# Row softmax on one core: two instruction-alignment directives moved behind the first pass, and the last two tiles divided and stored ahead of the next maximum

## The chip, the cores and the metric

One core of a Trainium2 chip runs the whole program. The metric is the device time of one execution in microseconds. The span of a profile (first to last event of the program) is about 1.8 us shorter than the time of the same execution: 315.6 against 317.42 us for the kernel before. A profile is of one execution, not of the median one.

## The reference

`x` is 32 x 512 x 1024 in float32, `temperature` is 0.5.

```python
scaled = x / temperature
shifted = scaled - np.max(scaled, axis=-1, keepdims=True)
exp_x = np.exp(shifted)
return (exp_x / np.sum(exp_x, axis=-1, keepdims=True)).astype(np.float32)
```

Each of the 16384 rows of 1024 numbers is read once and written once: 67.1 MB in, 67.1 MB out.

## The kernel before

The rows are cut into 16 tiles of 128 partitions x 8 rows (4.19 MB each), in six buffers. A tile is worked on in two groups of four rows. VectorE takes the maxima and later multiplies by the reciprocal of the sums; ScalarE takes the exponentials and sums them up as it goes; SyncE issues the loads, ScalarE's queue issues the stores. A buffer's next load is issued when its store has landed.

```python
def exponential(g): ...          # 4 activations on ScalarE, each with its row sums
def divide(g):
    nc.vector.reciprocal(recip, sums)
    for b in range(k):           # k = 4
        nc.vector.tensor_scalar_mul(
            tiles[i][:, a + b, :], in0=tiles[i][:, a + b, :], scalar1=recip[:, b : b + 1]
        )
def store(g):                    # only after a tile's second group
    ...
        nc.scalar.dma_start(out=dram(of, i)[:, a : a + k, :], in_=tiles[i][:, a : a + k, :])
        ... load()               # the tile six further on

with tc.manual_schedule():
    nc.vector.addr_align(128, offset=0, max_nops=0)
    nc.scalar.addr_align(128, offset=0, max_nops=0)
    for _ in range(BUFS):        # 6
        load()
    for g in range(len(groups) + 1):
        if g < len(groups):
            maximum(g)
            exponential(g)
        if g > 0:
            divide(g - 1)
            store(g - 1)
```

The division of a group stands behind the maximum of the next, so that ScalarE has its exponentials done by then. `addr_align` computes nothing: it asks that the next instruction of that engine lie at a multiple of 128 instruction slots. With `max_nops=0` the padding in front of it is jumped over.

Of the kernel before, what the change touches and what calls it, by code (L numbers as in the profile page):

```python
# [1 line left out]

# [4 lines left out]



TILES = [[8]] * 16  # L10
BUFS = 6

GROUP = 4


@with_exitstack
def kernel(
    ctx: ExitStack,
    tc: tile.TileContext,
    x: bass.AP,  # L20
    temperature: bass.AP,
    out: bass.AP,
):
    nc = tc.nc
    f32 = mybir.dt.float32
    scale = 1.0 / float(temperature)
    extreme = mybir.AluOpType.max if scale > 0 else mybir.AluOpType.min

    P = 128
    xf = x.flatten_outer_dims()  # L30
    of = out.flatten_outer_dims()
    n, d = xf.shape
    assert sum(sum(ks) for ks in TILES) * P == n

    data = ctx.enter_context(tc.tile_pool(name="data", bufs=BUFS))
    stats = ctx.enter_context(tc.tile_pool(name="stats", bufs=4))


    groups, first, r = [], [], 0
    for i, ks in enumerate(TILES):  # L40
        first.append(r)
        r += sum(ks)
        a = 0
        for k in ks:
            for b in range(0, k, GROUP):
                m = min(GROUP, k - b)
                groups.append((i, a + b, m, (a, k) if b + m == k else None))
            a += k

    def dram(t, i):  # L50
        k = sum(TILES[i])
        block = t[P * first[i] : P * (first[i] + k), :]
        return block.rearrange("(p k) d -> p k d", p=P, k=k)

    tiles, small = [], []

    def load():
        i = len(tiles)
        if i < len(TILES):
            xt = data.tile([P, sum(TILES[i]), d], f32, name="xt")  # L60
            nc.sync.dma_start(out=xt, in_=dram(xf, i))
            tiles.append(xt)

    def maximum(g):
        i, a, k, _ = groups[g]
        top, bias, sums, recip = (
            stats.tile([P, k], f32, name=name) for name in ("top", "bias", "sums", "recip")
        )
        small.append((bias, sums, recip))
        nc.vector.tensor_reduce(  # L70
            out=top, in_=tiles[i][:, a : a + k, :], axis=mybir.AxisListType.X, op=extreme
        )
        nc.vector.tensor_scalar_mul(bias, in0=top, scalar1=-scale)  # L73

    def exponential(g):
        i, a, k, _ = groups[g]
        bias, sums, _ = small[g]
        for b in range(k):
            nc.scalar.activation(  # L79
                tiles[i][:, a + b, :],  # L80
                tiles[i][:, a + b, :],
                mybir.ActivationFunctionType.Exp,
                bias=bias[:, b : b + 1],
                scale=scale,
                accum_out=sums[:, b : b + 1],
            )

    def divide(g):
        i, a, k, _ = groups[g]
        _, sums, recip = small[g]  # L90
        nc.vector.reciprocal(recip, sums)  # L91
        for b in range(k):
            nc.vector.tensor_scalar_mul(  # L93
                tiles[i][:, a + b, :], in0=tiles[i][:, a + b, :], scalar1=recip[:, b : b + 1]
            )

    def store(g):
        i, _, _, part = groups[g]
        if part:
            a, k = part  # L100
            nc.scalar.dma_start(out=dram(of, i)[:, a : a + k, :], in_=tiles[i][:, a : a + k, :])
            if a + k == sum(TILES[i]):
                load()



    with tc.manual_schedule():

        nc.vector.addr_align(128, offset=0, max_nops=0)
        nc.scalar.addr_align(128, offset=0, max_nops=0)  # L110
        for _ in range(BUFS):
            load()
        for g in range(len(groups) + 1):
            if g < len(groups):
                maximum(g)
                exponential(g)
            if g > 0:
                divide(g - 1)
                store(g - 1)


# [1 line left out]
_INS = ['x', 'temperature']  # L123
_OUTS = [((32, 512, 1024), 'float32')]

_NUMBERS = {'temperature': 0.5}


# [26 lines left out]
```

## Time and profile before

| | kernel before |
|---|---|
| median time | 317.71 us of 3 runs (317.61 to 318.15) |
| span of the profile | 315.6 us |
| VectorE busy | 235.5 us, 75% |
| ScalarE busy | 149.6 us, 47% |
| moved by DMA | 134.26 MB, 425 GB/s over the span |

How to read it: the two busiest engines leave a quarter and a half of the span idle, while the DMA row of the page stands at 90% or more in every slice but the first and the last. The queues tell what the bytes are:

```profile
DMA packets 4613, 134.26 MB, mean 425 GB/s; under 512 B 512, under 2 KB 512, under 8 KB 512
q1 hardware_dynamic: 2304, 67.11, 49.7%
q10 hardware_dynamic: 2304, 67.11, 49.2%
q14 instruction: 5, 0.04, 0.0%
```

The columns of a queue are packets, MB and the share of 16 DMA engines' time. q1 has the loads, q10 the stores. q14 is the fetch of the program's own instructions, five packets of 8 KB. They take 0.0% of the DMA engines' time.

### The profile page before, as it was taken

How to read it: one execution, taken by the hardware profiler on the slowest of the kernel's cores; microseconds unless marked ns; L12 is line 12 of the kernel's file. 1: busy time of each engine (PE TensorE's matmuls, PEld its weight loads, DVE VectorE, ACT ScalarE, POOL GpSimd, SP SyncE). 2: the span in 40 equal slices, each digit the busy share in tenths (PEclk: the TensorE clock that was granted, in tenths of full speed). 3: DMA queues.
4: the chain of work that ended last, by engine and by line, in shares of the span. 5: the costliest groups of instructions: out<-in, count | busy, mean ns of one | idle time of the engine just before them, and what ended most of it. 6: DMA issues, size and time to landing. Idle time of an engine off the chain costs nothing.

```text
span 315.6 us, 622 instructions
## 1 busy us (share of the span) xinstructions
DVE 235.5 (75%) x224; ACT 149.6 (47%) x257; POOL 0.2 (0%) x4
## 2 busy tenths in 40 slices
DVE  0299999999789494994939949498594976949720
ACT  0176666666626255361553615546065560645500
POOL 0000000000000000000000000000000000000000
DMA  8999999999999999999999999999999999999996
GB/s 330 415 448 415 386 457 407 461 411 453 424 440 432 432 432 429 444 424 453 415 454 407 457 407 457 403 461 403 461 403 461 403 462 403 461 419 444 428 436 278
DMA packets 4613, 134.26 MB, mean 425 GB/s; under 512 B 512, under 2 KB 512, under 8 KB 512
## 3 DMA queue, kind: packets, MB, share of 16 engines
q1 hardware_dynamic: 2304, 67.11, 49.7%
q10 hardware_dynamic: 2304, 67.11, 49.2%
q14 instruction: 5, 0.04, 0.0%
HBM read 67.11 MB, written 67.11 MB: 425 GB/s over the span
## 4 chain that ended last, share of the span: by engine, by line
DVE 72%; another core or an unknown queue 15%; DMA 4%; ACT 3%; issue 1%; DVEq 0%
DVE top L70 43%; DVE xt L93 27%; DMA xt<-in_x_dram 4%; ACT xt L79 3%; DVE recip L91 1%; DVE bias L73 1%; DVEq L150 0%
## 5 line engine op out<-in xcount | busy, mean ns | idle before, releaser
L79 ACT ACTIVATE xt<-xt,bias 128x1024 f32<-128x1024 f32 x128 | 145.4, 1137 | 136.0 <-DVE recip L91 118.6
L70 DVE TENSOR_REDUCE top<-xt 128x4 f32<-128x4096 f32 x32 | 141.3, 4416 | 62.2 <-DMA xt<-in_x_dram 62.2
L93 DVE TENSOR_SCALAR xt<-xt,recip 128x1024 f32<-128x1024 f32 x128 | 87.7, 749 | 1.1
L79 ACT ACTIVATION_READ_ACCUMULATOR xt<-xt,bias 128x1 f32 x128 | 23.8, 186 | 0.0
L79 ACT ACT_TABLE_LOAD x1 | 1.3, 1283 | 13.5 <-DMA xt<-in_x_dram 13.5
L91 DVE RECIPROCAL recip<-sums 128x4 f32<-128x4 f32 x32 | 5.5, 171 | 2.1 <-ACT xt L79 2.1
L73 DVE TENSOR_SCALAR bias<-top 128x4 f32<-128x4 f32 x32 | 5.5, 170 | 1.1
L136 POOL MEMSET const-bfloat16-1.0<- 128x1 bf16 x1 | 0.1, 102 | 0.0
L136 POOL MEMSET const-uint8-127<- 128x1 uint8 x1 | 0.1, 102 | 0.0
L136 POOL MEMSET const-float32-0.0<- 128x1 f32 x1 | 0.1, 99 | 0.2 <-issue 0.2
L136 POOL MEMSET const-float32-1.0<- 128x1 f32 x1 | 0.1, 99 | 0.0
## 6 DMA issues: line engine op xcount, KB each, us to landing
xt<-in_x_dram SPq DMA_DIRECT2D x16, 4096.0 KB, 50.2
out_dram<-xt ACTq DMA_DIRECT2D x16, 4096.0 KB, 38.4
```

Source lines behind the costliest of these rows:

```text
L70: nc.vector.tensor_reduce(out=top, in_=tiles[i][:, a : a + k, :], axis=mybir.AxisListType.X, op=extreme)
L73: nc.vector.tensor_scalar_mul(bias, in0=top, scalar1=-scale)
L79: nc.scalar.activation(tiles[i][:, a + b, :], tiles[i][:, a + b, :], mybir.ActivationFunctionType.Exp, bias=bias[:, b : b + 1], scale=scal ...
L91: nc.vector.reciprocal(recip, sums)
L93: nc.vector.tensor_scalar_mul(tiles[i][:, a + b, :], in0=tiles[i][:, a + b, :], scalar1=recip[:, b : b + 1])
L136: nc = _bacc.Bacc("TRN2", target_bir_lowering=False, num_devices=1)
```

## The change

The intent is twofold. The directives leave the head, where they stand ahead of all work, and come behind the first pass. And from tile 14 on, the second half of a tile is divided and stored before the next tile's maximum is taken: those stores go out earlier, and the last tile has no division between its two maxima.

```diff
+ALIGNED = 0
+ALONE = 14
...
     with tc.manual_schedule():
-        nc.vector.addr_align(128, offset=0, max_nops=0)
-        nc.scalar.addr_align(128, offset=0, max_nops=0)
         for _ in range(BUFS):
             load()
         for g in range(len(groups) + 1):
+            alone = g < len(groups) and groups[g][0] >= ALONE and groups[g][1] == 0
+            if g > 0 and alone:
+                divide(g - 1)
+                store(g - 1)
             if g < len(groups):
                 maximum(g)
                 exponential(g)
-            if g > 0:
+            if g > 0 and not alone:
                 divide(g - 1)
                 store(g - 1)
+            if g == ALIGNED:
+                nc.vector.addr_align(128, offset=0, max_nops=0)
+                nc.scalar.addr_align(128, offset=0, max_nops=0)
```

## The prediction

> **What bounds the kernel now.** I started with the page's time slices. The DMA row stands at 9 (90% or more) from the second slice to the next to last, while VectorE is 75% busy and ScalarE 47%. The DMA line under it gives 134.26 MB over the span, a mean of 425 GB/s, half read and half written. The first suspicion is therefore that transfers set the time and the engines only keep pace. Shares of busy time are averages, so I cut the trace into stretches at its two ends, each as long as one 4 MB tile takes (two calls; the columns are the stretch, its length, busy us of VectorE, ScalarE and GpSimd with counts, clock, DMA share, GB/s).
>
> ```profile
> DMA  8999999999999999999999999999999999999996
> ...
> 0.00:1.40 1.40, 0.00 (x0) 0.00 (x0) 0.20 (x4) 1.00 0.00 0
> 1.40:11.10 9.70, 0.00 (x0) 0.00 (x0) 0.00 (x0) 1.00 1.03 414
> 20.80:30.50 9.70, 9.38 (x11) 6.68 (x13) 0.00 (x0) 1.00 1.00 432
> 30.50:40.90 10.40, 10.33 (x12) 7.65 (x13) 0.00 (x0) 1.00 0.98 391
> 40.90:50.60 9.70, 9.63 (x8) 6.03 (x12) 0.00 (x0) 1.00 1.00 432
> ...
> 264.30:273.97 9.67, 9.60 (x8) 4.64 (x8) 0.00 (x0) 1.00 1.00 434
> 273.97:283.65 9.68, 5.12 (x8) 4.64 (x8) 0.00 (x0) 1.00 1.00 433
> 283.65:293.32 9.67, 9.60 (x8) 4.64 (x8) 0.00 (x0) 1.00 1.00 434
> 293.32:303.00 9.68, 6.64 (x12) 4.64 (x8) 0.00 (x0) 1.00 1.00 433
> 303.00:312.68 9.68, 0.00 (x0) 0.00 (x0) 0.00 (x0) 1.00 1.00 433
> 312.68:315.64 2.96, 0.00 (x0) 0.00 (x0) 0.00 (x0) 1.00 0.08 33
> ```
>
> What to see: the last column is 432 to 434 whether VectorE is busy 9.6 us of a stretch or not at all. A 4.19 MB tile, read or written, takes 9.67 us, and 32 such transfers in a row (16 loads, 16 stores) take 309.5 us. What the kernel spends above that is small: 1.4 us before the first byte, 0.7 us in the one slow stretch around the first store (10.4 instead of 9.7 us), some 0.5 us of slow start in the stretch before it at 414 GB/s, and some 3 us from the last byte to the span's end. The sum is 315 us, against a span of 315.6.
>
> Then the waits, to see whether the engines or the transfers are late:
>
> ```profile
> DVE top L70 <- DMA xt<-in_x_dram: 62.2, 12, 13.4
> ```
>
> VectorE stands idle for data 62.2 us in 12 waits; after the first (13.4 us) these are some 4.5 us, once per tile. The chain that ended last attributes 72% to VectorE, but it ends with the issue of the last store and follows VectorE back through its own instructions; it doesn't see that the transfers were full all the while. I trust the stretches over it.
>
> Last the tail, in order of time, because that is where the change acts:
>
> ```profile
> 262.90 4.42 DVE L70 TENSOR_REDUCE top<-xt 128x4 f32<-128x4096 f32 x1 [4.48 <-DMA xt<-in_x_dram]
> ...
> 270.41 0.34 ACTq L101 DMA_DIRECT2D out_dram<-xt  x1
> ...
> 282.25 4.42 DVE L70 TENSOR_REDUCE top<-xt 128x4 f32<-128x4096 f32 x1 [4.49 <-DMA xt<-in_x_dram]
> ...
> 289.76 0.34 ACTq L101 DMA_DIRECT2D out_dram<-xt  x1
> ...
> 302.01 0.34 ACTq L101 DMA_DIRECT2D out_dram<-xt  x1
> ```
>
> Tile 14 arrives at 262.9 and tile 15 at 282.25. The stores of tiles 13, 14 and 15 are issued at 270.41, 289.76 and 302.01. The completion records of the last four stores stand at 285.9, 295.5, 305.2 and 314.8: one every 9.6 to 9.7 us, the full rate. So when store 15 is issued at 302.01, store 14 still has 3.2 us to its completion. Store 15 completes 9.64 us after store 14: it followed without a gap. **This pair of numbers decides the prediction.**
>
> **The Trainium skill.** "DMA: Bandwidth & Descriptors", section Specifications, gives a fabric ceiling of 435 GB/s; the trace's 432 to 434 agrees, so no rearranged program moves these bytes faster. The same page, section "Queues, rings and completion order", says each DMA engine takes turns between the queues that have work, packet by packet. The trace agrees: the load and store queues have 49.7% and 49.2% of the engines' time, and with both filled a tile lands about every 19.4 us (262.9 to 282.25), twice 9.67. "Runtime: NRT & Kernel Launch", section "Instruction fetch mechanics", says instructions are refilled in 16 KiB blocks by DMA and that a taken branch out of the window stalls for a fetch. This trace shows 5 instruction packets with 0.04 MB in all, 8 KB each, so smaller pieces than the page's block; no view of the kernel before shows what such a branch costs.
>
> **The change, part by part.**
>
> *Alignment directives.* Two directives, one per engine, that compute nothing, move from ahead of all work to behind the first maximum and exponential. At the head their cost, if any, lies inside the 13.4 us wait for tile 0. In the new place VectorE meets its directive after the first bias (18.05 us) and ScalarE after its fourth exponential (22.6 us). What one costs there I can't read from this trace. From 13.4 to 84.8 us VectorE runs without a break and is behind the loads; a stall of d us moves the first store (33.1 us) by d. But six loads, 25.2 MB or 58 us of transfers, were queued at the start, so the transfers don't run dry; and VectorE catches up at its waits of 3.1 us (at 84.8) and then 4.5 us per tile. For d up to several us the cost is 0. Moving the directives may also move which engine fetches when, at about 0.3 us for one of 16 DMA engines: estimate 0 to 0.3 us either way.
>
> *Tiles 14 and 15: divide ahead of the maximum.* No instruction is added or removed; VectorE's order becomes max, divide, divide, max in place of max, divide, max, divide. Durations from the page's groups: maximum 4.42 (first after a wait) or 4.41, bias 0.17, reciprocal 0.17, four divisions 2.74 together; four exponentials 4.65 from the chain. Both reordered groups stand where VectorE idles 4.5 us for data.
> - Tile 13: its last exponentials run 255.66 to 260.3. Reciprocal and divisions follow at once, to 260.3 + 0.2 + 2.75 = 263.25; store 13 is issued about 263.3 and not at 270.41, 7.1 us earlier. The maximum of tile 14 starts at 263.3 instead of 262.9.
> - Tile 14: the two maxima end about 272.2, its exponentials at about 272.5 and 277.1, its second division at about 280.1. Store 14 is issued there, 9.6 us earlier than 289.76, and still before tile 15 lands, so the maximum of tile 15 starts at 282.25 as before.
> - Tile 15: between its two maxima there is no division now (0.17 + 2.74, minus small overlaps: 2.8 us). Second maximum 286.8 to 291.2, exponentials 287.0 to 291.5 and 291.5 to 296.1, last division to 299.2: store 15 issued about 299.2 and not 302.0, **2.8 us earlier**.
>
> On the path that sets the end: nothing. Store 13 joins a queue that still holds store 12 (until 285.9) and store 14 one that holds 12 and 13, so the DMA engines do the same work in the same order. Store 15 now waits about 6 us behind store 14 instead of 3.2, and completes at 314.8 again. Sum: 0 us from the reordering, -0.3 to +0.3 from the directives.
>
> **The rivals.**
> 1. *The tail is bound by compute.* Then the 2.8 us reach the end: 317.7 - 2.8 = 314.9, or 0.9% faster. For it: nothing but the long engine chain. Against it: the 433 GB/s stretch across 302 us and the 9.64 us between the last two completions.
> 2. *Earlier stores take bandwidth from the last loads.* Tile 15 would land later, at worst by part of the 7 us by which store 13 moves. Against it: the store queue wasn't empty at 263.3 in the kernel before, so it got its turn already; and even 3 us would be absorbed by the 2.8 us won.
> 3. *The directive stalls hard.* If an engine waits for a fetch through full DMA queues, each turn costs some 1.2 us (one 32 KB packet per engine at this rate, an estimate), so perhaps 2 to 6 us. VectorE has slack for this as shown; only over some 20 us would the transfers suffer. The end time would stay near 317.7.
> 4. *Fetch traffic shifts into or out of the tail.* A fetch of 0.3 us on the DMA engine that ends last moves the end by just that.
>
> **Range and chances.** The centre is the time before with a sliver off: 317.6. The three runs before spread over 0.54 us, and rivals 1 and 4 stretch the low side, a moderate stall and another chip the high side: 316.7 to 318.4. Faster by over 2% would need 6.4 us; above the 309.5 us of transfers there are only about 6 us in all, most of them start and completion. Slower by over 2% would need the transfers to stand idle 6.4 us, for which I see no mechanism but a very long stall. Chances 0.005, 0.985 and 0.01.
>
> **What would show it.** In the changed profile: stores issued near 263.3, 280.1 and 299.2 (reordering right); stretches to the end at 432 to 434 GB/s and the last two completions 9.6 to 9.7 us apart (bound right); tile 15 landing within 0.5 us of 282.25 (rival 2 wrong); an idle gap or none behind VectorE's 18 us and ScalarE's 22.6 us (cost of the directive), with the waits near 85 us shorter by that gap. I'd be wrong if the DMA share dropped in some slice after the first, or if the completion of the last store followed its issue by a constant 12.8 us, which would mean the tail had been the engines'.

## The result, and the profile after

The changed kernel takes 318.21 us (median of 6 runs, 317.52 to 318.31), the kernel before 317.60 us in the same rounds (6 runs, 317.43 to 318.15). The ratio is 1.0014 with a 95% interval of 1.0001 to 1.0027. Ratios here are the mean time of one kernel's runs over that of the other's of the same rounds, so they aren't quite the ratio of the medians quoted. Within 2% this is "the same"; the interval just leaves out 1, on the slow side.

Three views of the changed kernel answer those of the prediction. First the stretches (stretch, length, busy us of VectorE, ScalarE and GpSimd with counts, clock, DMA share, GB/s). A packet is counted whole in the stretch in which it starts, so a share of a short stretch can pass 1.00:

```profile
1.40:11.10 9.70, 0.00 (x0) 0.00 (x0) 0.00 (x0) 1.00 0.98 388
...
293.32:303.00 9.68, 5.05 (x9) 3.68 (x8) 0.00 (x0) 1.00 1.00 433
303.00:312.68 9.68, 0.00 (x0) 0.00 (x0) 0.00 (x0) 1.00 1.00 433
312.68:316.51 3.83, 0.00 (x0) 0.00 (x0) 0.00 (x0) 1.00 0.08 34
```

Up to 312.68 us the tail moves its bytes at 433 GB/s, as before. What has grown is the last row: 3.83 us in place of 2.96, at a share of 0.08. A share of 0.08 of 16 DMA engines says that on average little more than one of them was still at work. Then the tail in order of time:

```profile
263.92 4.41 DVE L74 TENSOR_REDUCE top<-xt 128x4 f32<-128x4096 f32 x1
264.04 0.34 ACTq L105 DMA_DIRECT2D out_dram<-xt  x1
...
280.81 0.34 ACTq L105 DMA_DIRECT2D out_dram<-xt  x1
283.12 4.42 DVE L74 TENSOR_REDUCE top<-xt 128x4 f32<-128x4096 f32 x1 [2.34 <-DMA xt<-in_x_dram]
287.65 4.41 DVE L74 TENSOR_REDUCE top<-xt 128x4 f32<-128x4096 f32 x1
300.02 0.34 ACTq L105 DMA_DIRECT2D out_dram<-xt  x1
```

The reordering works: the three stores go out at 264.0, 280.8 and 300.0, where they were at 270.4, 289.8 and 302.0. But tile 15 lands at 283.1, not 282.25. Third, a wait that the kernel before doesn't have (us in total, times, longest):

```profile
DVE top L74 <- issue: 0.4, 1, 0.4
```

That is VectorE at 17.75 us, where it meets its directive. ScalarE shows no such gap. The first store is still issued at 33.05 us (33.12 before), so the gap itself costs nothing. The views of `prof` leave branches out, but the packed traces have one branch record for each directive: at 0.72 and 0.76 us in the kernel before, at 17.59 us (VectorE) and 17.81 us (ScalarE) in the changed one, ten in the run `align_often` below, none in `no_align`, which has no directives.

**Following single DMA engines.** The last stretch asked which engine was late. The packet records give start, length and queue of each packet. In the steady part a DMA engine starts each 32 KB packet about 1.21 us after the one before, so I joined packets whose ends and starts meet into 16 chains, one per DMA engine. This is an inference, but a tight one: in all thirteen profiles the records can be joined so that each chain has 256 packets of 32 KB and, for each tile and queue, eight of them followed by one of 4 bytes. It shows:

- Before: 13 DMA engines end by 313.5 us, three at 314.3 to 314.5. Instruction packets after the start stand at 1.8, 3.6, 124.6, 162.3 and 253.3 us.
- After: 14 end by 313.7 us, two at 315.2 and 315.3. Instruction packets stand at 22.1, 22.1, 136.2, 163.1 and 260.2 us.
- An instruction packet of 8 KB holds its DMA engine for 0.31 us, and the data packet behind it is often slower, 1.33 to 1.82 us instead of 1.21. One fetch thus makes a DMA engine 0.4 to 0.9 us late. While the queues are full, that lag stays. Against the median of the 16, packet by packet, the latest DMA engine of the kernel before goes from 0.4 to 1.2 us at its fetch at 162.3 us and ends 1.2 us behind. In the changed kernel a DMA engine goes from 0.0 to 1.0 us at a fetch at 22.1 us, from 1.1 to 1.9 us at the one at 163.1 us, and ends 1.9 us behind.
- In every profile, whatever the kernel, the span ends 1.14 to 1.19 us after the last packet of a load or store on the latest DMA engine.

So the 0.87 us between the spans (316.51 and 315.64) are the lateness of one or two of 16 DMA engines. (The profile of the kernel before is of a run of 317.42 us, faster than each of the six timed ones, so the spans differ by more than the medians.) The experiments had to tell whether the moved fetches make it (theory A), or the early stores (theory B), or chance.

### The profile page after: what moved, and what is told of

It reads as the page before. It is cut to its first block, busy times and chain, and to the rows that moved or that the text cites. A ratio compares the mean times of both kernels' runs of the same rounds, so it can differ in the third digit from the quotient of the medians.

```text
span 316.5 us, 622 instructions
## 1 busy us (share of the span) xinstructions
DVE 235.8 (74%) x224; ACT 149.5 (47%) x257; POOL 0.2 (0%) x4
## 4 chain that ended last, share of the span: by engine, by line
DVE 69%; another core or an unknown queue 13%; ACT 7%; DMA 4%; issue 1%; DVEq 0%; ACTq 0%
DVE top L74 41%; DVE xt L97 25%; ACT xt L83 7%; DMA xt<-in_x_dram 4%; DVE bias L77 1%; DVE recip L95 1%; DVEq L160 0%; ACTq L83 0%
```

## The experiments

Eleven more runs were made, all of them correct and all within 2% of the kernel before. They came in three sets of rounds on three chips: the first four rows, the next four, the last three. Ratios are to be compared within a set first. The table has their times, each with the kernel before in the same rounds; the instruction packets of their profiles after 1 us; and the ends of the DMA engines.

| run | us (median, range) | before, us | ratio, 95% interval | instruction packets at us | most DMA engines end by; late ones |
|---|---|---|---|---|---|
| reorder_only | 317.78 (317.45 to 318.08) | 317.80 | 0.9998 (0.9986 to 1.0010) | 1.8, 3.9, 124.7, 162.7, 253.4 | 313.5; 314.5, 314.8 |
| align_only | 319.43 (318.21 to 321.14) | 317.80 | 1.0059 (1.0033 to 1.0085) | 22.1, 22.1, 136.9, 163.5, 260.9 | 314.3; 315.7, 316.0 |
| no_align | 317.90 (317.89 to 317.98) | 317.80 | 1.0003 (0.9991 to 1.0015) | 64.9, 65.0, 181.8, 240.1 | 313.8; 314.2, 314.8 |
| align_often | 321.08 (320.41 to 323.83) | 317.80 | 1.0124 (1.0093 to 1.0155) | ten: in pairs near 22, 66, 120, 180, 240 | 319.1; 320.9 |
| scalar_behind | 317.71 (317.65 to 318.06) | 317.65 | 1.0003 (0.9991 to 1.0015) | 4.1, 22.2, 135.7, 162.6, 259.7 | 313.5; 314.7, 314.8 |
| vector_behind | 318.54 (317.68 to 321.01) | 317.65 | 1.0042 (1.0015 to 1.0068) | 1.8, 22.2, 125.9, 165.5, 257.4 | 314.8; 318.1 |
| reorder_late | 317.96 (317.61 to 318.31) | 317.65 | 1.0008 (0.9996 to 1.0021) | as reorder_only | 313.7; 314.7, 315.0 |
| before_late | 317.96 (317.60 to 318.23) | 317.65 | 1.0007 (0.9995 to 1.0019) | as reorder_only | all 315.1 to 315.3 |
| before_later | 320.82 (320.70 to 321.26) | 317.82 | 1.0097 (1.0082 to 1.0113) | as reorder_only | all 317.8 to 317.9 |
| reorder_later | 317.90 (317.77 to 318.26) | 317.82 | 1.0004 (0.9991 to 1.0018) | as reorder_only | all 314.7 to 314.8 |
| after_again | 318.56 (318.16 to 318.57) | 317.82 | 1.0020 (1.0007 to 1.0032) | 22.0, 22.1, 136.6, 164.0, 263.0 | 313.8; 314.1, 314.9, 315.6 |

### One half of the change at a time

`reorder_only` is the changed kernel with the directives back at the head:

```diff
     with tc.manual_schedule():
+        nc.vector.addr_align(128, offset=0, max_nops=0)
+        nc.scalar.addr_align(128, offset=0, max_nops=0)
...
-            if g == ALIGNED:
-                ...
```

> Only the order of VectorE at tiles 14 and 15 is changed; the directives stay at the head. Theory A (the 0.6 to 0.9 us that the changed kernel lost come from where instruction fetches fall among the transfers, and the reordering is hidden): ratio 1.000, 317.6 us, last store issued 2 to 3 us ahead of 302.0 but completed at 314.8 again, fetches near 1.8, 3.6, 125, 162 and 253 us as in the kernel before. Theory B (the reordering costs it: stores 13 and 14 come early and disturb the last loads): 318.2 us and tile 15 landing near 283.1 instead of 282.2.

Measured: 0.9998, with the last store issued at 299.53 us. The reordering alone costs nothing and gains nothing in time. Theory B falls. Tile 15 lands at 282.6 in its profile; three profiles with the old order and the directives at the head (the kernel before, before_late, before_later) have 282.2, 283.0 and 282.7.

`align_only` has the moved directives and the old order:

```diff
-ALONE = 14
+ALONE = 99
```

> Only the two directives are moved behind the first pass; the order of VectorE is that of the kernel before. Theory A: 318.2 us (+0.6, as the changed kernel has), two fetches near 22 us, and tile 2 landing some 0.35 us later than in the kernel before. Theory B: 317.6 us.

Measured: 1.0059, more than the whole change, and single runs up to 321.1 us. Theory A holds in direction, but its size was too small. (Tile 2 landed 0.35 us later as expected, at 32.71 us by the packet records, but so it did in `reorder_only`, so that sign tells nothing.) The tail shows two things. A late DMA engine delays the landing of tile 15 (283.8 us), since VectorE starts on it only when the last of 16 completion records is there (in the kernel before at 282.23 us, VectorE at 282.25); with the old order the last store is then issued at 303.57 us, when most DMA engines are just running dry. In the packet records its first packets start at 304.43, and the other engines end at 314.2 to 314.3, a microsecond later than in the kernel before. So fourteen DMA engines wait for the store, by up to a microsecond. But the two late ones never wait, and it is they that end the span, at 315.7 and 316.0 us: the profile (a run of 318.99 us) shows more lateness, not a cost of the waiting.

`no_align` has the old order and no directives (`ALIGNED = -1`).

> No directives at all, order of the kernel before. Theory A: the time depends only on where the fetches fall, so between 317.2 and 318.3 us, and the fetches tell which: with at most two of them after 30 us on one DMA engine about 317.6. A rival for the directives' purpose (they keep an engine from stalling in its stream) expects idle time of an engine that the kernel before doesn't have, and over 318.5 us.

Measured: 1.0003, and no idle time of an engine that the kernel before lacks. At this resolution the directives at the head buy nothing. The run also parts the fetch from the jump: there is no jump in it, and yet the lags of two DMA engines rise by 0.3 to 0.9 us at their fetches, and these two end last.

`align_often` gives the dose: the pair of directives behind five passes.

```diff
-            if g == ALIGNED:
+            if g in (0, 6, 12, 18, 24):
```

> The dose: the two directives stand behind the passes 0, 6, 12, 18 and 24, order of the kernel before. Theory A: each further directive adds a branch over padding and one or two 8 KB fetches per engine, each delaying the DMA engine that carries it by 0.4 to 0.8 us (309 ns plus a slower packet behind it, from the packet records); with four more on the same engine the end moves by 1.5 to 3 us, to 319.5 to 321 us, with all other DMA engines ending as before near 313.2 us. A rival (the fetches are absorbed, and the 0.6 us are something else): 317.6 to 318.3 us.

Measured: 1.0124, 321.08 us. The queue of instructions and the tail (first the queue, then stretches in the columns used above), from the profile of the slowest of the six runs, 323.83 us:

```profile
q14 instruction: 10, 0.08, 0.1%
```

```profile
296.00:302.00 6.00, 5.93 (x6) 3.24 (x7) 0.00 (x0) 1.00 1.02 437
302.00:305.00 3.00, 1.45 (x3) 3.00 (x5) 0.00 (x0) 1.00 0.81 350
305.00:308.00 3.00, 2.60 (x5) 0.33 (x2) 0.00 (x0) 1.00 0.46 197
308.00:311.00 3.00, 0.32 (x1) 0.00 (x0) 0.00 (x0) 1.00 0.82 350
```

Ten instruction packets where there were five, and a hole in the transfers near 308 us, with a first one near 296 that these rows don't cover. The DMA engine with four fetches after 60 us is so late that tile 15 lands at 288.6 us; the stores of tiles 14 and 15 then come at 296.1 and 308.35, and nearly all DMA engines stand idle for two to three us ahead of each. I had expected the other DMA engines to end as before, near 313.2. They end at 319.1, because lateness of one reaches all of them through the landing of a load, the engines' work on that tile, and the issue of its store. The late one itself, with five fetches, never waits, and ends the span at 320.9. Not all of its lateness is fetches: it also has slow load packets, 1.3 to 2.0 us, with no fetch ahead of them.

### How late may the last store be?

Three scalings by 1.0 ahead of the last divisions delay the last store:

```diff
         nc.vector.reciprocal(recip, sums)
+        if g == len(groups) - 1:
+            for b in range(3):
+                nc.vector.tensor_scalar_mul(
+                    tiles[i][:, a + b, :], in0=tiles[i][:, a + b, :], scalar1=1.0
+                )
```

> Directives at the head, new order, and three scalings by 1.0 (0.75 us each, 2.25 us) ahead of the very last divisions, so that the last store is issued that much later. Theory (the reordering gives the last store slack and nothing else): with the order alone it was issued at 299.5, its first packet could start 0.86 us later and was needed at 303.4, so 3.0 us were spare; 2.25 us more are hidden: ratio 1.000 to the kernel before. Rival (the last store's issue sets the end): +2.2 us, 320 us.

> The same three scalings in the kernel before. Theory: its last store was issued at 302.0, could start at 302.9 and was needed at 303.4, so 0.5 us are spare; 2.25 us more leave the DMA engines dry for 1.7 us: 319.3 us, ratio 1.004 to 1.006. Rival (no difference of the two orders in slack): the same ratio as the run with the new order.

Measured: 1.0008 and 1.0007. The first was expected, the second missed by 1.3 us. The three scalings delayed the store by 1.7 us, and in `before_late` the DMA engines did run dry, as the stretch shows (the kernel before first, then `before_late`):

```profile
302.00:305.00 3.00, 0.00 (x0) 0.00 (x0) 0.00 (x0) 1.00 1.19 513
...
302.00:305.00 3.00, 2.42 (x4) 0.00 (x0) 0.00 (x0) 1.00 0.46 197
305.00:308.00 3.00, 0.00 (x0) 0.00 (x0) 0.00 (x0) 1.00 1.20 513
```

Yet all 16 then ended together, at 315.1 to 315.3 us. Fourteen waited 1.3 to 2.1 us for nothing, because they would only have ended ahead of the late ones. What I had left out was this second slack. A longer delay had to tell it from others: eight scalings, `range(2 * k)` over the four rows twice.

> Eight scalings by 1.0 instead of three ahead of the last divisions of the kernel before, 5.3 us (the three moved the store by 1.7 us, 0.66 each). Theory (the end is set by the one DMA engine that lags some 1.2 us, or by the last store where that comes later than both): last store issued about 307.9, first packets 0.86 us later, 9.7 us of transfer, all DMA engines ending together near 318.5: 321 to 321.5 us, +1.1%. Rival (the delay was hidden for another reason than lag): under 319.

> The same eight scalings with the new order and the directives at the head. Theory: last store issued about 305.1, first packets at 306.0, so the DMA engines run dry for 2.6 us but the lagging one ends near 315.2 anyway: 318.2 to 319 us, 2.5 to 3 us under the run with the old order, which is what the reordering is worth once the store is late. Rival (the order gives no slack): the same time as the old order, 321.

Measured: 1.0097 (320.82 us) and 1.0004 (317.90 us), both a little under the ranges expected: the eight scalings moved the store by 4.7 us and not 5.3. The same delay costs the old order 3.0 us and the new one nothing. In the tails (old order first, then new) one sees why:

```profile
302.00:305.00 3.00, 3.00 (x6) 0.00 (x0) 0.00 (x0) 1.00 0.48 208
305.00:308.00 3.00, 2.14 (x4) 0.00 (x0) 0.00 (x0) 1.00 0.00 0
308.00:311.00 3.00, 0.00 (x0) 0.00 (x0) 0.00 (x0) 1.00 1.23 524
```

```profile
302.00:305.00 3.00, 2.04 (x4) 0.00 (x0) 0.00 (x0) 1.00 0.71 306
305.00:308.00 3.00, 0.00 (x0) 0.00 (x0) 0.00 (x0) 1.00 0.98 415
308.00:311.00 3.00, 0.00 (x0) 0.00 (x0) 0.00 (x0) 1.00 0.81 350
```

With the old order the store goes out at 307.17 and the transfers stand still for more than 3 us. With the new order it goes out at 304.08, the gap is 0.8 to 1.7 us on fourteen DMA engines, and all 16 DMA engines end at 314.7 to 314.8, where the late one would have ended in any case. The reordering is thus worth 3 us of slack, of which the kernel with its directives at the head uses none.

### Which directive?

`scalar_behind` and `vector_behind` are the changed kernel with only one directive behind the first pass, the other at the head.

> The changed kernel with only the directive of ScalarE behind the first pass, that of VectorE at the head. Theory (ScalarE's stream carries the fetches near 125 and 253 us, which become 136 and 260, and the moved directive adds one more near 22 us on the DMA engine that already has two): nearly the whole loss, 318.0 to 318.4 us, one fetch near 22 us. If VectorE's directive is the costly one: 317.6 to 317.8.

> The changed kernel with only the directive of VectorE behind the first pass, that of ScalarE at the head. Theory: one fetch near 18 to 22 us and one near 163, on a DMA engine with none else; 317.6 to 317.9 us, the 0.4 us gap of VectorE at 17.75 us still there. If VectorE's directive is the costly one: 318.0 to 318.4.

Measured: 1.0003 and 1.0042, the reverse of what I expected. ScalarE's stream does carry the fetches that move from 125 and 253 to 136 and 260 us, and one more appears near 22 us, but the time is that of the kernel before. The ends of the DMA engines show why: the one with ScalarE's fetches ends at 314.8 us in place of 314.5 in `reorder_only`, but the one with VectorE's ends at 314.8 there already. VectorE's directive costs: single runs from 317.68 to 321.01, and its profile, that of a 321.01 us run, has the clearest late DMA engine of all (the kernel before first, then `vector_behind`).

```profile
311.00:314.00 3.00, 0.00 (x0) 0.00 (x0) 0.00 (x0) 1.00 0.51 218
314.00:317.00 3.00, 0.00 (x0) 0.00 (x0) 0.00 (x0) 1.00 0.00 0
...
311.00:314.00 3.00, 0.00 (x0) 0.00 (x0) 0.00 (x0) 1.00 0.83 360
314.00:317.00 3.00, 0.00 (x0) 0.00 (x0) 0.00 (x0) 1.00 0.08 33
```

By 314.8 us fifteen DMA engines are done; one goes on until 318.1. It is the one whose chain carries VectorE's fetches at 22.2 and 165.5 us. Two fetches account for some 1.7 us of its lateness of 4.0 us behind the median (twice 0.31, and packets of 1.80 and 1.75 behind them in place of 1.21). The rest comes from slow data packets, all of them loads, of 1.34 to 2.08 us, which that chain shows about once per tile between 59 and 156 us. Why it falls out of step with the others, and whether this goes with VectorE's directive rather than ScalarE's or with single runs, one profile doesn't tell.

These two runs also show whose fetches are whose. The fetches at 4.1 and 162.6 us that stay when ScalarE's directive moves are VectorE's, and they lie on one DMA engine; those of ScalarE (22.2, 135.7 and 259.7) lie on another. In the ten profiles whose ends the last store doesn't set, the DMA engine that ends last is always one of these two. (Lateness has other sources too: of the three late ones in the kernel before, the one at 314.3 us carries no fetch.) In both profiles of the changed kernel it is ScalarE's, at 315.3 and 315.6 us, with VectorE's at 315.2 and 314.9. So with both directives moved both DMA engines are late, and the loss can't be put down to VectorE's directive alone.

### Once more

`after_again` is the changed kernel unaltered.

> The changed kernel once more, to see whether its +0.14% is there in other rounds. Theory (fetches during the stream make one or two DMA engines late, by an amount that differs from run to run): median 317.9 to 318.5, single runs from 317.5 up to 319 or more, never under the kernel before. Rival (it was chance): ratio 1.000 with the spread of the kernel before.

Measured: 1.0020, no run under 318.16 us, with the median of 318.56 just above the range expected. The loss is unlikely to be chance: two sets of rounds give 1.0014 and 1.0020, both with intervals above 1.

No version here beats both kernels. `reorder_only`, the changed kernel with its directives left at the head, equals the kernel before and has the 3 us of slack besides.

## Why the prediction was right or wrong

**The bound.** Right: the transfers set the time, and the 9.7 us stretches of the tail stand at 433 to 434 GB/s up to 312.68 us in both kernels. But the reading was too coarse. I took "433 GB/s to the end, last two completions 9.64 us apart" as proof that there was slack to spare. In the kernel before, the last store's data was needed at 303.4 us by most DMA engines, and could start 0.86 us after the issue at 302.0: 0.5 us to spare, not the 3.2 us that I read from the completion of store 14. Completions are set by the latest DMA engine, so they overstate the slack of the others: of the 16 completion records of store 15, twelve stand at 313.4 to 313.7 us, and the last at 314.8. Nor are the "some 3 us from the last byte to the span's end" what they were read as: data packets run until 314.47, and 1.17 us follow.

**The reordering.** Right in its mechanism. The stores were expected at 263.3, 280.1 and 299.2 us and came at 264.0, 280.8 and 300.0, each 0.7 to 0.8 us late, as VectorE starts on tiles 13 and 15 0.72 and 0.87 us later. Its effect on the time was expected as 0 and is 0.9998. Its effect on slack was called 6 us in place of 3.2 and is 2.6 in place of 0.5, counted from the packets (303.49 - 300.02 - 0.86 in the changed kernel).

**The directives.** This is the term that was mis-sized: "estimate 0 to 0.3 us either way". Measured on the whole change, the medians are 0.61 and 0.74 us apart in the two sets of rounds, and the two spans 0.87 and 1.15 us above that of the kernel before. ScalarE met its directive at 17.81 us by the branch record, not at 22.6. I counted only the fetch, 0.3 us on one of 16 DMA engines, which the packet records confirm at 0.31. I didn't count the slow data packet behind it (up to 0.6 us more), nor that an engine's lateness stays and adds up, nor that it delays the landing of every load from then on. With the old order that term alone was 1.6 us by the medians (align_only). Whether the reordering paid for the difference isn't shown: the two were never run in the same rounds, single runs of align_only go from 318.21 to 321.14, and in its profile the late DMA engines didn't wait for the store.

**The rivals.** Rival 1, a tail bound by compute, is false for both kernels, but by less than I thought: in `align_only` and `align_often` most DMA engines already wait for the last store, and in `before_later` it sets the end. Rival 2, stores taking the loads' turns: tile 15 did land 0.9 us later in the changed kernel, past the 0.5 us that I had named as the sign, but `reorder_only` (282.6) and `align_only` with its old order (283.8) speak against the early stores as its cause. Rival 3, a hard stall: false, the gap at VectorE's directive is 0.4 us and the first store isn't later. Rival 4, fetch traffic that reaches the end, is what happened, two to two and a half times as large by the medians as the 0.3 us that I gave it.

**The range.** 318.21 us lies in 316.7 to 318.4. The sign of the small rest was wrong: centre 317.6, a sliver under the time before, measured a sliver over.

## What to carry to other kernels

When DMA sets the time, ask which of the 16 DMA engines ends last, not only what the sum moves: here a rate of 433 GB/s hid one or two late ones, which set the landing of the loads and the end, while the others had slack. Look where an edit moves or adds instruction fetches: in these runs each one in the stream of transfers made a DMA engine 0.3 to 1.0 us late, and the lag stayed. Test a hidden reordering by delaying what it moved: equal times at rest hid 3 us of slack that showed under a delay of 4.7 us.

## What the Trainium skill lacked or had wrong

- "Runtime: NRT & Kernel Launch", section "Instruction fetch mechanics", has refills of 16 KiB whose boundary cost is "mostly hidden". In these runs each instruction packet has 8,192 bytes and comes singly (124.6, 162.3, 253.3 us in the kernel before); it holds a DMA engine for 0.31 us and, after 20 us, is followed by a data packet of 1.32 to 1.82 us in place of 1.21 (54 of 55 fetches). Whether the smaller piece is a setting of this machine, no run shows. Hidden from VectorE and ScalarE, yes; from a kernel bound by its transfers, no: where ten packets stood in place of five, the median was 3.3 us longer (align_often).
- The same section names the stall of a taken branch without a size. Here VectorE's jump over padding (a branch record of 47 ns) left a gap of 0.4 us, ScalarE's none. No instruction packet lies in that gap, the next ones start at 22.1 us, so these runs don't show that the gap is this stall.
- "DMA: Bandwidth & Descriptors", section "Latency and other measured facts", gives about 0.6 us to the first byte for such queues. From the start of a store's issue record, itself 0.34 us long, to its first packet on idle DMA engines it was 0.84 to 0.86 us in align_only, before_late, before_later, reorder_later and align_often. The page doesn't say from where it counts, so the two may measure different things.
- No page gives the time from the last packet of a store on the latest DMA engine to the end of the span: 1.14 to 1.19 us in every profile here. And none says that instruction fetches make single DMA engines late for good: the latest one ends up to 3.3 us behind the next (vector_behind).
